# Low parts of streamed weight tiles: a negated copy and an accumulating DMA in place of a subtraction

## The chip, the cores and the metric

The kernel runs on one core of a Trainium2 chip. The metric is the device time in microseconds of one execution; the median of three runs before the change is 2350.99 us (2349.08 to 2353.13).

The engines are named as in the profile: PE (TensorE, the matmuls), PEld (its weight loads), DVE (VectorE), ACT (ScalarE), POOL (GpSimd), SP (SyncE, which only issues DMAs). Each engine works through its own instructions in program order. A DMA is issued by an engine and then moved by the core's 16 DMA engines.

## What is computed

One inference step of a two-layer backbone on 640 tokens (128 context, 512 latent) of width 2048. Each layer is

```python
h = x * (1 + scale) + shift              # modulation by the conditioning vectors
z = h @ w_in_l                           # 2048 x 6656, split into 12 parts
att    = windowed attention(aq, ak, av, sink, cached context)
hg_out = bidirectional gated scan(hq, hi, hff, hfb)
cv_out = silu(layer_norm(depthwise_conv31(ca * sigmoid(cb))))
mix = concat([att * silu(ag), hg_out * silu(hgate), cv_out * silu(cgate)])
out = mix @ w_out_l                      # 2048 x 2048
x_new = layer_norm(ALPHA * x + gate * out, ln_w_l, ln_b_l)
```

and the modulation vectors come from `silu(cond) @ ada_w + ada_b`. All data are float32.

## The kernel before, in words

**Matmuls in three products.** PE multiplies in the type `float32r`. To keep the precision of float32, each operand is held as a high part (the value cast to `float32r`) and a low part (the value less the high part), and three products are added in PSUM: high by high, high by low, low by high. The activations are kept so in `HH` and `HL`; the weights are streamed, and each streamed tile is split when it has arrived.

**The weight stream.** `w_in` comes as 52 column tiles per layer, 128 output columns each, and each of these as four quarters of 128 x 512 (256 KB). `w_load1` takes one of eight raw slots (`raw`) and has SP load a quarter into it; `w_split` takes two of sixteen slots (`wh`), lets ACT write the high part (line 285) and DVE or POOL subtract it from the raw quarter to get the low part (line 286), and gives the raw slot back. `mm` then does the matmuls of a quarter: four blocks of 128 rows, three products, each on 256 and on 384 tokens (lines 1161 and 1163). `o_load` and `o_split` do the same for the 64 tiles of `w_out` per layer.

**The order.** Python generators (the attention, the scan, the convolution, the modulation of later steps) stand in a list, and `pump` advances them a few steps between matmul quarters, so that each engine's instruction order is fixed when the program is built. In the loop over column tiles `i`, after the matmuls of quarter `c`, `ahead(i, c)` splits quarter `c` of tile `i + 1` and loads up to three quarters beyond it. So a quarter is split about three quarters of a tile's matmuls before PE needs it. Before, `ahead` gave the subtraction to POOL for odd quarters and for all quarters while 32 <= i < 46, and to DVE otherwise; `o_split` always used DVE.

**The stages of a layer**, in the order in which PE meets them: the tiles of the scan (four rounds of `hg_main`, whose products are on lines 534 to 567), of the attention (`att`, lines 856 to 942), of the convolution (`e_ca` with 31 taps on DVE, line 1021, then `conv_ln` with its sums over partitions on lines 420 and 421), the gates, and the output projection (line 1413), in groups of 512 output columns. At the start of the output projection POOL loads the residual `Y` with five DMAs of 1 MB (line 1273; `y0y` in layer 0, `y1y` in layer 1). They can start only when the memory of the mixing stage is free. In layer 1, `rows` also has POOL multiply `Y` by the LayerNorm weight and add its bias, group by group (line 1292). Beside all this, DVE computes the modulation of the next steps as row products (`ada_dve`, line 356), whose tiles come through the same raw slots.

In the output projection `feed` splits tile n as soon as the slots of tile n - 8 are free; tiles 0 to 3 are split while PE is still at the last column tile, and tiles 4 to 6 before the first product.

Of the kernel before, what the change touches and what calls it, by code (L numbers as in the profile page):

```python
# [9 lines left out]
F32 = mybir.dt.float32  # L10
# [3 lines left out]
AF = mybir.ActivationFunctionType  # L14
ALU = mybir.AluOpType
# [5 lines left out]
T = 640  # L21
# [68 lines left out]
class Slots(Free):  # L90
    """SBUF slots whose tile is made anew when its type changes."""

# [32 lines left out]
def trunk(ctx: ExitStack, tc: tile.TileContext, A: dict):  # L125
    nc = tc.nc
    act, dve, pool, pe, sync = nc.scalar, nc.vector, nc.gpsimd, nc.tensor, nc.sync
# [74 lines left out]

# [1 line left out]
    sync.dma_start(out=sm, in_=A["small"])  # L204
# [32 lines left out]

# [1 line left out]
    active = []  # L239
# [41 lines left out]
    def split(hi, lo, src, lo_eng=None, hi_eng=None):  # L281
        if hi_eng:
            hi_eng.tensor_copy(hi, src)
        else:
            act.copy(hi, src)  # L285
        (lo_eng or dve).tensor_tensor(lo, src, hi.bitcast(F32), op=ALU.subtract)  # L286

# [1 line left out]
    def adab(l, part):  # L289
        o = SM["adab"] + 48 * l + 16 * part  # L290
        return sm[:, o:o + 16]
# [88 lines left out]

# [1 line left out]
    xq = deque()  # L382
# [16 lines left out]

# [1 line left out]
    act.activation(nsink, sm[:, SM["sink"]:SM["sink"] + 16], AF.Copy, scale=-1.0)  # L401
# [9 lines left out]

# [1 line left out]
    CH = (slice(0, 384), slice(384, T))  # L413
# [10 lines left out]

# [1 line left out]
    HGS = Free([0, 1])  # L426
# [292 lines left out]

# [1 line left out]
    kvres = {}  # L721
# [268 lines left out]

# [1 line left out]
    convs = {}  # L992
# [114 lines left out]

# [1 line left out]
    wraw = {}  # L1109
# [13 lines left out]
    def w_split(l, i, c, lo_eng=None, hi_eng=None):  # L1123
        pump_until(lambda: len(WH.f) >= 2)
        hi, lo = WH.take(), WH.take()
        r = wraw.pop((l, i, c))
        split(hi, lo, r, lo_eng, hi_eng)
        wsp[l, i, c] = (hi, lo)
        RAW.put(r)
# [11 lines left out]
    def o_split(l, t):  # L1141
        pump_until(lambda: len(WH.f) >= 2)
        hi, lo = WH.take(), WH.take()
        r = oraw.pop((l, t))
        split(hi, lo, r)
        osp[l, OT[t][0], OT[t][1]] = (hi, lo)
        RAW.put(r)

# [1 line left out]
    def mm(l, i, z, ks, halves):  # L1150
# [13 lines left out]

# [1 line left out]
    NS = 3  # L1166
# [39 lines left out]
    for l in range(DEPTH):  # L1206
# [16 lines left out]
        first = NS if l == 0 else 2  # L1223
        wnext = 4 * (first + 2)

        def ahead(i, c):
            nonlocal wnext
            m = 4 * (i + 1) + c
            if i + 1 < NN:
                w_split(l, i + 1, c, pool if c % 2 or 32 <= i < 46 else None)  # L1230
            else:
                o_split(l, c)
            while wnext <= m + (WLH if 0 in hold else WLA):
                if wnext < 4 * NN:
                    w_load1(l, wnext // 4, wnext % 4)
                else:
                    o_load(l, wnext - 4 * NN)
                wnext += 1
# [17 lines left out]

# [1 line left out]
        for k in range(KT):  # L1258
# [143 lines left out]
        for gi, (n0c, w) in enumerate(GROUPS[:-1]):  # L1402
# [3 lines left out]
            for k0 in range(0, KT, 2):  # L1406
                for tts, k in [(p, k) for p in ((range(3), range(3, TT)) if k0 == 0 else (range(TT),))
                               for k in (k0, k0 + 1)]:
                    hi, lo = osp[l, gi, k // kper]
                    o = w * (k % kper)  # L1410
                    for tt in tts:
                        for n_, (h_, w_) in enumerate(((HH, hi), (HH, lo), (HL, hi))):
                            pe.matmul(bs[tt][:, 0:w], lhsT=h_[:, tt, k, :], rhs=w_[:, o:o + w],  # L1413
                                      start=(k == 0 and n_ == 0), stop=(k == KT - 1 and n_ == 2))
# [28 lines left out]
        for tt in range(TT):  # L1443
            b = banks.popleft() if last else obank[tt]
            for k in range(KT):
                hi, lo = osp[l, gi, k // 2]
                o = w * (k % 2)
                for n_, (h_, w_) in enumerate(((HH, hi), (HH, lo), (HL, hi))):
                    pe.matmul(b[:, 0:w], lhsT=h_[:, tt, k, :], rhs=w_[:, o:o + w],
                              start=(k == 0 and n_ == 0), stop=(k == KT - 1 and n_ == 2))  # L1450
# [133 lines left out]
```

## Time and profile before

| | |
|---|---|
| median of the runs | 2350.99 us |
| span of the profiled execution | 2354.9 us |
| PE busy | 2211.0 us (94%) |
| PE weight loads busy | 2101.6 us (89%) |
| DVE busy | 1788.6 us (76%) |
| ACT busy | 894.0 us (38%) |
| POOL busy | 718.6 us (31%) |
| mean granted TensorE clock | 0.976 |

The profiled execution spans 2354.9 us, 3.9 us above the median of the runs. The shares are means over stages with different limits; which engine is waited for is read stage by stage. Issuing a DMA does not count as busy.

### The profile page before, as it was taken

To read this page: it belongs to the slowest core of one execution; us is meant where nothing else is said; L and a number is where in the kernel's file an instruction comes from. 1 tells how busy PE (TensorE), PEld (TensorE's weight loads), DVE (VectorE), ACT (ScalarE), POOL (GpSimd) and SP (SyncE) were. 2 spreads that over 40 slices of the span, in tenths; PEclk is the share of its full clock that TensorE was granted. 3 is DMA by queue.
4 is the path that set the end of the run, shared out by engine and by line. 5 is a ranking of instruction groups with operands and counts; after the bars stand their busy time and mean duration, and the time that the engine had idled before them with its cause. 6 is when DMAs were issued, how large, how long until landed. Compare 5 with 4: busy or idle time off the path is not lost.

```text
span 2354.9 us, 41512 instructions
## 1 busy us (share of the span) xinstructions
PE 2211.0 (94%) x15854; PEld 2101.6 (89%) x15854; DVE 1788.6 (76%) x3890; ACT 894.0 (38%) x1647; POOL 718.6 (31%) x540
## 2 busy tenths in 40 slices
PE   6898989999999986999998999999999999999996
PEld 3598989998999986978898999999999999998886
DVE  3488899778869999976576788886776799856547
ACT  1165655423443221431125466653344421251111
POOL 0034244321223444300003343343222255524125
PEclk9999999999999998999999999999999999999998
DMA  9933343443432233564433233333333132335333
GB/s 368 396 118 124 113 126 114 138 138 108 127 95 81 95 103 102 154 235 149 131 117 126 90 106 107 94 103 116 108 104 93 53 97 63 95 92 190 103 88 114
DMA packets 151351, 298.67 MB, mean 127 GB/s; under 512 B 17936, under 2 KB 23792, under 8 KB 149232
## 3 DMA queue, kind: packets, MB, share of 16 engines
q1 hardware_dynamic: 138992, 271.85, 36.0%
q10 hardware_dynamic: 9920, 12.10, 1.7%
q0 software_dynamic: 2240, 12.08, 1.3%
q8 instruction: 124, 2.03, 0.4%
q14 instruction: 75, 0.61, 0.1%
HBM read 278.61 MB, written 12.11 MB: 123 GB/s over the span
## 4 chain that ended last, share of the span: by engine, by line
PE 40%; DVE 25%; issue 3%; ACT 2%; DMA 0%; POOL 0%; ACTq 0%; SPq 0%; DVEq 0%; POOLq 0%
PE z L1163 12%; DVE s L1021 11%; PE z L1413 8%; PE z L1161 8%; PE m L1413 7%; DVE junk L356 5%; DVE wh L286 1%; PE m L856 1%; PE m L942 1%; DVE s L528 1%; DVE y1y L1382 1%; DVE s L527 1%; ACT s L1360 1%; DVE y1y L1383 0%; ACT wh L285 0%
## 5 line engine op out<-in xcount | busy, mean ns | idle before, releaser
L1163 PE MATMUL z<-HH,wh 128*128 128x384 f32 x3296 | 1055.9, 341 | 0.0
L1161 PE MATMUL z<-HH,wh 128*128 128x256 f32 x3296 | 934.7, 285 | 10.8 <-DVE s L1010 6.5
L286 POOL TENSOR_TENSOR wh<-raw,wh 128x512 fp32r<-128x512 f32 x256 | 387.1, 1519 | 893.2 <-ACT wh L285 637.8
L1161 PEld LDWEIGHTS z<-HH,wh 128*128 128x128 f32 x3296 | 627.9, 191 | 15.5 <-issue 5.0
L356 DVE SCALAR_TENSOR_TENSOR junk<-raw,s 128x256 bf16<-128x256 f32 x1024 | 617.1, 603 | 26.1 <-DMA raw<-adawD 4.0
L1163 PEld LDWEIGHTS z<-HH,wh 128*128 128x128 f32 x3296 | 627.2, 190 | 1.5
L1163 PE MATMUL z<-HL,wh 128*128 128x384 f32 x1648 | 561.9, 341 | 0.0
L285 ACT CAST wh<-raw 128x512 fp32r<-128x512 f32 x536 | 319.6, 617 | 520.1 <-PE m L1413 135.7
L286 DVE TENSOR_TENSOR wh<-raw,wh 128x512 fp32r<-128x512 f32 x288 | 260.7, 916 | 287.2 <-ACT wh L285 283.3
L1161 PE MATMUL z<-HL,wh 128*128 128x256 f32 x1648 | 465.2, 282 | 0.0
L1161 PEld LDWEIGHTS z<-HL,wh 128*128 128x128 f32 x1648 | 315.3, 191 | 0.0
L1163 PEld LDWEIGHTS z<-HL,wh 128*128 128x128 f32 x1648 | 313.5, 190 | 0.0
L1021 DVE SCALAR_TENSOR_TENSOR s<-s,sm,s 128x655 f32<-128x655 f32 x240 | 288.4, 1202 | 6.3
L1413 PE MATMUL z<-wh,HH 128*128 128x512 f32 (+1 forms) x768 | 207.8, 357 | 7.3 <-ACT s L1090 5.5
L1413 PEld LDWEIGHTS z<-wh,HH 128*128 128x128 f32 x768 | 137.3, 191 | 28.4 <-ACT s L1090 5.8
L1413 PE MATMUL m<-wh,HH 128*128 128x512 f32 (+1 forms) x512 | 150.9, 376 | 0.0
L1413 PE MATMUL z<-wh,HL 128*128 128x512 f32 (+1 forms) x384 | 136.8, 356 | 0.0
L1413 PEld LDWEIGHTS m<-wh,HH 128*128 128x128 f32 x512 | 94.2, 188 | 17.7
L1413 PE MATMUL m<-wh,HL 128*128 128x512 f32 (+1 forms) x256 | 96.2, 376 | 0.0
L1292 POOL TENSOR_TENSOR y1y<-y1y,s 128x2560 f32<-128x2560 f32 (+1 forms) x10 | 48.4, 4838 | 120.7 <-DMA s<-lnw_r 104.5
L356 DVE DVE_READ_ACCUMULATOR junk<-raw,s 128x1 f32 x1024 | 82.8, 81 | 0.0
L1413 PEld LDWEIGHTS z<-wh,HL 128*128 128x128 f32 x384 | 73.3, 191 | 10.3
(553 smaller groups left out, 2577.9 us busy)
## 6 DMA issues: line engine op xcount, KB each, us to landing
raw<-win SPq DMA_DIRECT2D x416, 256.0 KB, 2.7
raw<-adawD SPq DMA_DIRECT2D x256, 256.0 KB, 2.7
x<-adaw SPq DMA_DIRECT2D x64, 512.0 KB, 8.3
raw<-wout SPq DMA_DIRECT2D x128, 256.0 KB, 2.8
s<-crow SPq DMA_DIRECT2D x32, 256.0 KB, 4.0
s<-xT ACTq DMA_DIRECT2D x16, 320.0 KB, 7.3
s<-s ACTq DMA_DIRECT2D x80, 64.0 KB, 2.1
y0y<-xr POOLq DMA_DIRECT2D x5, 1024.0 KB, 10.9
```

Of the source, the lines that this page charges most:

```text
L285: act.copy(hi, src)
L286: (lo_eng or dve).tensor_tensor(lo, src, hi.bitcast(F32), op=ALU.subtract)
L356: dve.scalar_tensor_tensor(junk, r[:, 256 * n:256 * n + 256], 1.0, rows[0][:, 256 * c:256 * c + 256], op0=ALU.mult, op1=ALU.mult, accum_ou ...
L527: dve.tensor_tensor(o, o, cap(Kt, 0, [[T + h, 2], [2 * h, nb], [1, h]]), op=ALU.mult)
L528: dve.scalar_tensor_tensor(er[:, 0:T], er[:, 0:T], SC, q, op0=ALU.mult, op1=ALU.mult)
L856: pe.matmul(b[:, 0:w], lhsT=a_, rhs=k_, start=(n_ == 0), stop=(n_ == 2))
L942: pe.matmul(o, lhsT=v_, rhs=p_, start=(y == 0 and n_ == 0), stop=(y == len(bl) - 1 and n_ == 2))
L1021: dve.scalar_tensor_tensor(acc, u[:, t:t + AW], sm[:, cw + t:cw + t + 1], acc, op0=ALU.mult, op1=ALU.add)
L1161: pe.matmul(za, lhsT=w_, rhs=h_[:, 0:2, k, :], start=st_, stop=sp_)
L1163: pe.matmul(zb, lhsT=w_, rhs=h_[:, 2:5, k, :], start=st_, stop=sp_)
L1292: pool.tensor_tensor(yv, yv, s[:, 0:w].unsqueeze(1).to_broadcast([P, TT, w]), op=op)
L1413: pe.matmul(bs[tt][:, 0:w], lhsT=h_[:, tt, k, :], rhs=w_[:, o:o + w], start=(k == 0 and n_ == 0), stop=(k == KT - 1 and n_ == 2))
```

## The change

`split_add` is new. ACT writes the high part as before, then writes the negated high part into the low slot, and POOL issues a DMA that adds the raw tile to what stands there. It is used for every quarter that `ahead` splits and for every tile of `w_out`: 516 tiles. The 28 quarters that are split elsewhere (16 at the start of layer 0, 12 between the layers) keep the subtraction.

```diff
+    def split_add(hi, lo, r):
+        act.copy(hi, r)
+        act.activation(lo, hi.bitcast(F32), AF.Copy, scale=-1.0)
+        pool.dma_start(out=lo.bitcast(F32), in_=r, accum_op=ALU.add)
...
-        split(hi, lo, r, lo_eng, hi_eng)
+        if lo_eng == "dma":
+            split_add(hi, lo, r)
+        else:
+            split(hi, lo, r, lo_eng, hi_eng)
         wsp[l, i, c] = (hi, lo)
...
         r = oraw.pop((l, t))
-        split(hi, lo, r)
+        split_add(hi, lo, r)
         osp[l, OT[t][0], OT[t][1]] = (hi, lo)
...
             if i + 1 < NN:
-                w_split(l, i + 1, c, pool if c % 2 or 32 <= i < 46 else None)
+                w_split(l, i + 1, c, "dma")
             else:
                 o_split(l, c)
```

What this does to the order is seen on two engines. On POOL, at the start of layer 1's output projection, before the change (`a10v` and `a10k` are tiles of the mixing stage, `y1y` is the residual):

```order
L1097 TENSOR_TENSOR a10v<-a10v,s_12476 128x640
L286 TENSOR_TENSOR wh_17546<-raw_246,wh_621 128x512
L286 TENSOR_TENSOR wh_239<-raw_250,wh_238 128x512
L1273 DMA y1y<-n_107 128x2048 x5
L1292 TENSOR_TENSOR y1y<-y1y,s_19266 128x5x512
L1292 TENSOR_TENSOR y1y<-y1y,s_19268 128x5x512
```

and at the same place after it (line 291 is the accumulating DMA, lines 1281 and 1300 are the former 1273 and 1292):

```order
L291 DMA wh_413<-raw_164 128x512
L291 DMA wh_234<-raw_516 128x512
L291 DMA wh_417<-raw_166 128x512
L1281 DMA y1y<-n_107 128x2048 x5
L291 DMA wh_618<-raw_248 128x512
L291 DMA wh_17947<-raw_246 128x512
L291 DMA wh_17980<-raw_518 128x512
L1300 TENSOR_TENSOR y1y<-y1y,s_19725 128x5x512
L1300 TENSOR_TENSOR y1y<-y1y,s_19727 128x5x512
L291 DMA wh_239<-raw_250 128x512
L291 DMA wh_7542<-raw_162 128x512
```

POOL had nothing of the weights behind the five loads of the residual; now the low parts of tiles 4, 5 and 6 (the three rows under `y1y<-n`) are issued behind them, and those of tile 7 and later behind the two passes over the residual as well. In layer 0 the loads of `y0y` stand ahead of the same tiles, without the passes.

On ACT, in a round of the scan in layer 0, before the change:

```order
L285 CAST wh_416<-raw_164 128x512
L651 COPY s_117<-m_103 128x512
L651 COPY s_133<-m_104 128x512
L285 CAST wh_617<-raw_166 128x512
L661 COPY s_141<-m_101 128x128
```

and at the same place after it (line 289 is the cast, line 290 the negated copy; the copies out of PSUM on lines 656 and 666 are the former 651 and 661):

```order
L289 CAST wh_416<-raw_164 128x512
L290 ACTIVATE wh_417<-wh_416 128x512
L656 COPY s_117<-m_103 128x512
L656 COPY s_133<-m_104 128x512
L289 CAST wh_617<-raw_166 128x512
L290 ACTIVATE wh_618<-wh_617 128x512
L666 COPY s_141<-m_101 128x128
```

Behind each cast ACT has a second instruction of the same size, which waits for the first, and the copies of the scan, which stood behind the cast, now stand behind both.

## Rows read from the trace of the kernel before

**Rows 1.** The page, section 1: the span.

```profile
span 2354.9 us, 41512 instructions
```

**Rows 2.** Windows: length; busy (x) of PE, PEld, DVE, ACT, POOL; PEclk, DMA, GB/s.

```profile
150.00:420.00 270.00, 241.65 (x2240) 236.40 (x2239) 247.31 (x597) 152.74 (x246) 96.58 (x77) 0.95 0.39 119
420.00:740.00 320.00, 311.68 (x2111) 307.89 (x2110) 246.67 (x731) 124.11 (x286) 81.42 (x65) 0.98 0.38 115
740.00:965.00 225.00, 194.07 (x1278) 190.99 (x1277) 218.81 (x413) 50.36 (x87) 93.63 (x75) 0.94 0.32 102
965.00:1025.00 60.00, 54.48 (x352) 53.25 (x351) 56.90 (x179) 27.19 (x43) 12.95 (x8) 0.96 0.55 171
...
1310.00:1580.00 270.00, 263.99 (x2486) 260.49 (x2486) 225.67 (x416) 166.63 (x270) 112.23 (x89) 1.00 0.34 102
```

**Rows 3.** Windows, one of 50 us in layer 1's convolution stage, same columns.

```profile
1950.00:2000.00 50.00, 50.00 (x343) 50.00 (x342) 48.62 (x39) 11.09 (x20) 32.50 (x20) 1.00 0.21 64
```

**Rows 4.** Waits of PE: instruction, whom it waited for, us in total, times, longest.

```profile
PE m L534 <- DVE s L601: 19.5, 10, 3.4
PE m L420 <- ACT s L285: 13.5, 1, 13.5
...
PE m L856 <- DVE ats L871: 8.7, 4, 4.0
...
PE z L1161 <- POOL wh L286: 1.5, 3, 0.5
```

**Rows 5.** Groups by line: form, count, busy us, mean ns, idle before and its releasers.

```profile
L286 POOL TENSOR_TENSOR wh<-raw,wh 128x512 fp32r<-128x512 f32 x256 | 387.1, 1519 | 893.2 <-ACT wh L285 637.8 <-PE z L1163 156.0 <-issue 66.6
L285 ACT CAST wh<-raw 128x512 fp32r<-128x512 f32 x536 | 319.6, 617 | 520.1 <-PE m L1413 135.7 <-PE z L1413 132.1 <-DMA raw<-win 125.9
...
L286 DVE TENSOR_TENSOR wh<-raw,wh 128x512 fp32r<-128x512 f32 x288 | 260.7, 916 | 287.2 <-ACT wh L285 283.3 <-DMA s<-gsc 2.7 <-issue 0.5
...
L874 ACT ACTIVATE wh<-wh,ats 128x512 f32<-128x512 f32 (+2 forms) x50 | 30.4, 609 | 110.0 <-DVE ats L871 110.0
```

**Rows 6.** Timeline of DVE around 1926 to 1952 us: start, length, instructions merged.

```profile
1925.72 17.60 DVE L1021 SCALAR_TENSOR_TENSOR s<-s,sm,s 128x655 f32<-128x655 f32 x11
...
1946.44 5.58 DVE L1021 SCALAR_TENSOR_TENSOR s<-s,sm,s 128x655 f32<-128x655 f32 x6
```

**Rows 7.** Timeline of POOL in the same stretch, up to its last instruction there.

```profile
1927.71 7.50 POOL L286 TENSOR_TENSOR wh<-raw,wh 128x512 fp32r<-128x512 f32 x4 [8.41 <-ACT wh L285]
...
1935.30 5.48 POOL L286 TENSOR_TENSOR wh<-raw,wh 128x512 fp32r<-128x512 f32 x3
1940.94 1.68 POOL L286 TENSOR_TENSOR wh<-raw,wh 128x512 fp32r<-128x512 f32 x1 [0.17 <-ACT wh L285]
```

**Rows 8.** Line 286 on POOL from 740 to 920 us: durations in ns (min/median/max).

```profile
L286 POOL TENSOR_TENSOR wh<-raw,wh x42: 1275/1406/2004, 743.0 to 915.8; 128x512 fp32r<-128x512 f32 x42
```

**Rows 9.** The same line on POOL from 150 to 420 us.

```profile
L286 POOL TENSOR_TENSOR wh<-raw,wh x27: 1277/1469/1983, 161.3 to 411.1; 128x512 fp32r<-128x512 f32 x27
```

**Rows 10.** DMA issues: queue, count, KB each, median us from issue to landing.

```profile
raw<-win SPq DMA_DIRECT2D x416, 256.0 KB, 2.7
...
s<-s ACTq DMA_DIRECT2D x80, 64.0 KB, 2.1
```

**Rows 11.** Line 1273 (POOL's loads of the residual): durations in ns, then landing.

```profile
L1273 POOL DMA_DIRECT2D y0y<-xr x5: 540/540/594, 1032.2 to 1034.4; - x5
...
DMA to landing us min/median/max: 5.7/10.9/16.9
```

**Rows 12.** Timeline of POOL in layer 1's output projection.

```profile
2116.89 2.73 POOL L1273 DMA_DIRECT2D y1y<-n  x5 [26.98 <-issue]
2135.41 11.86 POOL L1292 TENSOR_TENSOR y1y<-y1y,s 128x2560 f32<-128x2560 f32 x2 [15.78 <-DMA y1y<-n]
```

**Rows 13.** The chain, stretches 1010 to 1060 and 2105 to 2140: start, length, work.

```profile
1037.20 2.72 PE z L1413 x12
...
2125.93 2.72 PE z L1413 x12
```

## Prediction

> **What bounds the kernel now.** I read the windows by stage first, then PE's waits, then the other engines in the stretches where PE waits. The profiled execution spans 2354.9 us [rows 1], 3.9 us above the median of the runs (2350.99); the sum below is made against the span and then moved down by those 3.9 us. In most of layer 1 PE is the limit: in a convolution stretch it is busy for 50.00 of 50 us although DVE is at 48.62 [rows 3]. What can be won stands in layer 0 [rows 2]: PE is idle for 28.4 of 270 us in the scan (150 to 420), 8.3 of 320 in the attention, 30.9 of 225 around the convolution, 5.5 of 60 before the output projection, and 6.0 of 270 in layer 1's scan: 79 us. PE's waits say for whom [rows 4]: in the scan DVE (line 601 above all), in the attention DVE (line 871), and after the convolution the cast of line 285, which waits for the last taps. DVE is busy for 247 of 270, 247 of 320 and 219 of 225 us in the three stretches. The granted clock is 0.95, 0.98 and 0.94 there, and 1.00 in layer 1's scan: between its two levels, 1.2 and 2.4 GHz, some 67 us pass at the lower one, next to the idle times.
>
> **What DVE gets back.** Of its 288 subtractions 266 go, at 916 ns [rows 5]: 244 us. POOL loses 250 of 256, at 1519 ns. That second removal matters for DVE too. In layer 1's convolution six taps in a row take 5.58 us, 0.93 each, when POOL is still; eleven taken just before, while POOL makes eight subtractions, take 17.60 us, 1.60 each [rows 6, 7]. 17.60 less 11 x 0.93 is 7.4 us, so a subtraction on POOL makes DVE about 0.9 us slower. From 740 to 920 us POOL makes 42 of them [rows 8]: 39 us of slowing, so DVE's 219 us at the convolution become 180 of 225 (80%). From 150 to 420 it makes 27 [rows 9], worth 25 us, and as even quarters go to DVE, as many of DVE's own go, another 25: 197 of 270 (73%). In layer 1's scan DVE is busy for 226 of 270 us (84%) and PE idle for only 6 [rows 2], so PE should there become the limit. I take 26 of 28.4 us in layer 0's scan, 25 of 30.9 at the convolution (some latency remains behind the last tap), 5 of 8.3 in the attention, 3 of 5.5 before the projection, 2 of 6.0 in layer 1's scan, where ACT gets fuller. With 7 us for time at the lower clock that goes with the gaps (33 at most: half of 67), the gain is 68 us; its bounds are 0 and 79 + 33.
>
> **What is added.** ACT gets 516 negated copies. The nearest rows are its cast, 617 ns, and an activation of the same size, 609 ns [rows 5]: 315 us, from 894 to about 1,210, 51% of the span. POOL gets 516 issues at 540 ns [rows 11], less than the subtractions took. The accumulating DMA itself no row shows. Below: a 256 KB load lands after 2.7 us, and 64 KB from SBUF to SBUF after 2.1 [rows 10]. Above: 1 MB lands after 5.7 us when nothing is ahead of it [rows 11]. It has to read source and target, so I take 4 us, the middle, and keep 2.7 and 8.
>
> The Trainium skill (Collectives: The Full Stack, "The bandwidth ceiling: the fold count and why AG ≠ RS ≠ AR") says that a reducing DMA is slower only because it reads two sources, not for the addition. No run here shows it. By that page the moving part would double: 64 KB more cost (2.7 - 2.1) / 3 = 0.2 us, so 256 KB would land at about 3.5 us, an estimate, and the sum would be about 1 us better.
>
> **What hides it.** A column tile is 96 matmuls; at 343 in 50 us [rows 3] that is 14.0 us. A quarter is split three quarters of a tile ahead, 10.5 us. Cast, copy, issue and landing make 0.6 + 0.6 + 0.5 + 4 = 5.7 us, so 4.8 us are left for waits in queues. Before, half of the quarters already stood in POOL's queue behind the scan's and the attention's work, and PE waited 1.5 us in all for POOL's low parts [rows 4]. I put 4 us on new waits of this kind, and 1 us on the four copies ahead of the projection's casts on ACT.
>
> **Where it isn't hidden.** At the start of the output projection POOL issues the five residual loads and, behind them, the low parts of tiles 4 to 6. The loads are issued within 2.7 us but land after 5.7, 10.9 (median) and 16.9 us [rows 11, 12]: one after the other, about 2.8 us each. A DMA that POOL issues behind them will land behind them. In layer 0 the last load is issued at 1034.4, so the data are there at about 1051, tile 4's low part at about 1053; PE starts tile 4 at 1037.20 and needs it 0.2 us later [rows 13]. That is a wait of 15 us; since the loads wait for DVE's last gate, which will be less late, I take 13. In layer 1 the passes over the residual start when its loads have landed, at 2135.41 [rows 12], so tile 4's low part is there at about 2137, and PE starts it at 2125.93 [rows 13]: 11 us. The passes then hold POOL until 2147.3, so tile 7's low part lands at 2147.3 + 0.5 + 4 = 2151.8; at 3.4 us per tile (15 matmuls at 2.72 / 12 us) PE would want it at 2136.3. Together 15 us. What is late next: nothing, since the slots of the tiles behind have come free meanwhile. The later passes, 12 us for each group, are queued when PE is at the group's ninth tile, and the low part behind them is wanted eight tiles, 27 us, later: covered. Long waits lower the clock: in the stretch with the 13.5 us for line 285 it is 0.94, 27 of 225 us at the lower level [rows 2, 4], more than the wait itself; I take 5 us for both. The last tiles, split only when the eighth tile before them is done and then used in quick succession, cost 1 us per layer. Loss: 13 + 15 + 5 + 2 + 4 + 1 = 40 us.
>
> **Sum.** 68 - 40 = 28 us: a span of 2327, a median of 2323 us. Its own range, with half of the unsure shares of the gain (20 us) and the landing between 2.7 and 8 us: 2303 to 2345.
>
> **The rivals.**
> - *The waits at the projections are not there* (accumulating DMAs get past the loads, or the mixing stage ends so much earlier that the loads are through). Against: the five landings in turn, and in layer 1 DVE was not late, so nothing ends earlier. Then of the losses 7 us remain: 2351 - 68 + 7 = 2290. The Trainium skill (DMA: Bandwidth & Descriptors, "SWDGE vs HWDGE vs iDMA") says that only one queue is allocated to the DMAs that GpSimd issues; by that rule the first half of this rival cannot happen, and the landings agree.
> - *Gains and losses meet*: the scan of layer 0 keeps most of its idle time because its steps wait for each other, not for DVE's load. 2323 + 26 = 2349.
> - *ACT becomes the limit of the scan* (slower). A round of the scan has 16 splits, so ACT gets 9.8 us more per round, in line with its exponentials and copies out of PSUM; in layer 1 it goes from 167 of 270 us to about 205 [rows 2]. If half of it lies on the chain, 5 us in each of eight rounds, layer 0 gains 20 us less and layer 1 loses 22 more: 2365. From 3.5 us per round on, the change loses. For it: casts wait for raw tiles, and a raw slot now comes free some 3 us later, so ACT waits in order too. Against: ACT is still idle for a quarter of the stage.
> - *The accumulating DMA is slow* (slower): if its packets take so long that a tile needs more than PE's 3.4 us in the output projection, PE waits at some 120 tiles; at 5.4 us per tile this is 240 us, 2560. If only its landing is late, 8 us instead of 4, the two waits grow by 4 each and some quarters at the end of layer 0's convolution, which are split late, cost about 10: 2341; it decides from about 12 us.
>
> **Chances.** The forecast 0.55, no waits at the projections 0.10, gains and losses meet 0.08, ACT as the limit 0.15, a slow DMA 0.12. A measurement of this kernel tells about 0.2% (4.7 us) from no change: faster 0.65, same 0.08, slower 0.27. The range reaches down to the first rival and up past ACT's half case: 2285 to 2390.
>
> **What the profile will show.** Right: layer 0's scan and convolution with PE idle for under 10 us each, DVE near 80%, and the taps at 0.93 us almost throughout; two waits of PE of 10 to 16 us for an accumulating DMA, one soon after each start of the output projection, and a second piece in layer 1 behind line 1300. ACT near 1,210 us. Wrong: PE waiting for ACT in the scan's rounds; accumulating DMAs that land after more than 8 us away from the residual loads; or no wait at the residual loads, in which case the time is below 2303.

## The result and the profile after

The changed kernel takes 2296.7 us in the median (four runs, 2296.3 to 2298.2), the kernel before 2350.95 on the same chip: ratio 0.9765, 95% interval 0.9753 to 0.9777, 54 us less. The forecast was 2323, with 2303 to 2345 as its own range: the direction is right, and the gain is about twice the 28 us foreseen. The time lies below that range, and inside the 2285 to 2390 that the forecast kept open for its rivals.

The page of the changed kernel, its span and the engines' busy time (share of the span, instructions):

```profile
span 2295.2 us, 42650 instructions
...
PE 2187.4 (95%) x15854; PEld 2081.0 (91%) x15854; DVE 1369.6 (60%) x3624; ACT 1217.7 (53%) x2163; POOL 753.5 (33%) x806
```

The profiled spans differ by 59.7 us (2354.9 [rows 1] to 2295.2). DVE is busy for 1,370 us instead of 1,789. ACT is at 1,217.7, where 1,210 was expected. On POOL the issues of the accumulating DMAs do count as busy in this view: they are 453.9 of its 753.5 us (below).

Windows of the changed kernel, with the columns of [rows 2]. Both kernels give PE the same instructions in the same order, so each window begins at the PE instruction that begins the stage before:

```profile
148.56:385.73 237.17, 229.05 (x2238) 225.47 (x2238) 208.94 (x553) 185.40 (x297) 94.90 (x103) 1.00 0.76 189
385.73:695.41 309.68, 306.64 (x2110) 303.90 (x2110) 203.47 (x716) 174.05 (x368) 84.85 (x96) 0.99 0.76 184
695.41:881.34 185.93, 185.93 (x1278) 185.88 (x1277) 175.79 (x403) 79.25 (x134) 63.54 (x80) 1.00 0.80 193
881.34:943.36 62.02, 54.12 (x350) 52.96 (x350) 50.03 (x172) 36.29 (x58) 16.05 (x17) 0.94 0.89 237
943.36:1080.84 137.48, 127.39 (x550) 104.64 (x548) 51.84 (x184) 50.60 (x83) 37.27 (x45) 0.96 0.92 234
...
1244.48:1509.46 264.98, 263.34 (x2486) 260.38 (x2485) 152.47 (x368) 207.59 (x333) 110.35 (x121) 1.00 0.70 163
...
2036.51:2079.96 43.45, 32.47 (x138) 26.10 (x138) 6.93 (x10) 17.50 (x30) 23.73 (x18) 0.88 0.73 211
```

Read against [rows 2] (length less PE's busy time is its idle time; the bounds of those rows moved by up to 0.25 us to the same PE instructions): layer 0's scan takes 237.2 us instead of 269.9 with 8.1 idle, the attention 309.7 instead of 320.0 with 3.0 idle, the convolution 185.9 instead of 225.1 with no idle time at all, layer 1's scan 265.0 instead of 269.9. PE's clock is 1.00, 0.99 and 1.00 in layer 0's three stages, where it was 0.95, 0.98 and 0.94. The fourth row is the first that loses: 62.0 us up to the start of layer 0's output projection, before 60.1.

For the projections' first stretches, which had no row yet, the kernel before, same columns:

```profile
1025.25:1150.14 124.89, 124.89 (x549) 103.31 (x548) 78.90 (x230) 25.75 (x42) 2.73 (x5) 0.99 0.53 179
...
2110.07:2140.05 29.98, 29.98 (x139) 25.14 (x139) 15.20 (x19) 10.50 (x18) 7.37 (x6) 1.00 0.68 264
```

The first 125 us of layer 0's projection became 137.5, the rest up to layer 1's tiles 163.6 (160.0), and the stretch in which layer 1's projection starts 43.5 (30.0); in between, 3.0 us were won in 530. With 1.6 us won ahead of the first row and 0.4 lost behind the last, 91.7 us were won and 32.0 lost.

PE's waits in the changed kernel, to be read against [rows 4]:

```profile
PE z L1421 <- DMA wh<-raw: 20.4, 3, 9.7
...
PE z L1421 <- ACT s L1095: 8.1, 2, 7.9
...
PE m L539 <- DVE s L606: 4.6, 5, 1.4
```

The waits for DVE's lines 606 and 876 (601 and 871 before) fell from 19.5 to 4.6 and from 8.7 to 3.0 us, and the one for the sums behind the convolution is gone. New are three for an accumulating DMA (`wh<-raw`), and 8.1 us for ACT's line 1095, the last gate.

The groups by line of POOL's new issues, DVE's row products of the modulation, and its taps (count | busy us, mean ns | idle before), then the latter two of the kernel before:

```profile
L291 POOL DMA_DIRECT2D wh<-raw x516 | 453.9, 959 | 1352.3 <-ACT wh L290 1243.1
...
L361 DVE SCALAR_TENSOR_TENSOR junk<-raw,s 128x256 bf16<-128x256 f32 x1024 | 506.6, 495 | 172.2 <-DMA raw<-adawD 141.8
...
L1026 DVE SCALAR_TENSOR_TENSOR s<-s,sm,s 128x655 f32<-128x655 f32 x240 | 224.3, 935 | 6.3
```

```profile
L356 DVE SCALAR_TENSOR_TENSOR junk<-raw,s 128x256 bf16<-128x256 f32 x1024 | 617.1, 603 | 26.1 <-DMA raw<-adawD 4.0
...
L1021 DVE SCALAR_TENSOR_TENSOR s<-s,sm,s 128x655 f32<-128x655 f32 x240 | 288.4, 1202 | 6.3
```

A tap took 1,202 ns in the mean before, a row product 603. Both are faster now, where the forecast had measured taps alone. POOL's issues take 0.86 us in the median (below), not 0.54, and 453.9 us together, more than the 387.1 of the subtractions [rows 5].

The accumulating DMAs up to layer 0's output projection (durations of the issue in ns, then issue to landing), and the landing of the three that are issued behind the residual loads there:

```profile
L291 POOL DMA_DIRECT2D wh<-raw x195: 849/860/1868, 132.4 to 929.0; - x195
...
DMA to landing us min/median/max: 3.2/4.6/8.5
...
DMA to landing us min/median/max: 14.8/15.5/16.3
```

The timeline of POOL at the start of layer 0's projection and of its passes over the residual in layer 1, and PE's first instruction after the first wait (start, length, in brackets the idle time before):

```profile
947.10 2.65 POOL L1281 DMA_DIRECT2D y0y<-xr  x5 [17.20 <-issue]
949.74 2.71 POOL L291 DMA_DIRECT2D wh<-raw  x3
...
2061.16 11.46 POOL L1300 TENSOR_TENSOR y1y<-y1y,s 128x2560 f32<-128x2560 f32 x2 [11.04 <-DMA y1y<-n]
```

```profile
964.58 0.80 PE L1421 MATMUL z<-wh,HH 128*128 128x512 f32 x1 [9.70 <-DMA wh<-raw]
```

This is the forecast mechanism: five loads, then three accumulating DMAs, the first of which is issued at 949.74 and lands 14.8 us later, when PE goes on. In layer 1 line 1300 then holds POOL for 11.46 us, to 2072.6, and PE waits for a second piece, 1.6 us.

### The profile page after: what moved, and what is told of

Read it like the earlier page. It is cut to its first block, busy times and chain, and to the rows that moved or that the text cites. A ratio compares the mean times of both kernels' runs of the same rounds, so it can differ in the third digit from the quotient of the medians.

```text
span 2295.2 us, 42650 instructions
## 1 busy us (share of the span) xinstructions
PE 2187.4 (95%) x15854; PEld 2081.0 (91%) x15854; DVE 1369.6 (60%) x3624; ACT 1217.7 (53%) x2163; POOL 753.5 (33%) x806
## 4 chain that ended last, share of the span: by engine, by line
PE 70%; DVE 10%; issue 7%; DMA 7%; ACT 3%; POOL 2%; ACTq 0%; SPq 0%; POOLq 0%; DVEq 0%
PE z L1171 32%; PE z L1169 21%; PE z L1421 5%; PE m L1421 4%; DVE junk L361 4%; DMA x<-adaw 2%; PE m L947 2%; PE m L861 2%; POOL wh L291 1%; DMA wh<-raw 1%; DMA s<-xT 1%; PE m L915 1%; DVE HL L286 1%; DMA raw<-win 1%; PE m L663 1%
## 5 line engine op out<-in xcount | busy, mean ns | idle before, releaser
L1171 PE MATMUL z<-HH,wh 128*128 128x384 f32 x3296 | 1045.4, 338 | 0.0
L1169 PE MATMUL z<-HH,wh 128*128 128x256 f32 x3296 | 924.7, 282 | 0.9 <-DVE wh L286 0.9
L291 POOL DMA_DIRECT2D wh<-raw x516 | 453.9, 959 | 1352.3 <-ACT wh L290 1243.1
L1169 PEld LDWEIGHTS z<-HH,wh 128*128 128x128 f32 x3296 | 618.2, 188 | 4.4 <-DVE wh L286 1.6
L1171 PEld LDWEIGHTS z<-HH,wh 128*128 128x128 f32 x3296 | 619.4, 188 | 1.5
L361 DVE SCALAR_TENSOR_TENSOR junk<-raw,s 128x256 bf16<-128x256 f32 x1024 | 506.6, 495 | 172.2 <-DMA raw<-adawD 141.8
L290 ACT ACTIVATE wh<-wh 128x512 fp32r<-128x512 f32 x516 | 326.4, 632 | 73.7 <-PE z L1171 59.0
L1169 PEld LDWEIGHTS z<-HL,wh 128*128 128x128 f32 x1648 | 310.2, 188 | 0.0
L1171 PEld LDWEIGHTS z<-HL,wh 128*128 128x128 f32 x1648 | 309.9, 188 | 0.0
L1026 DVE SCALAR_TENSOR_TENSOR s<-s,sm,s 128x655 f32<-128x655 f32 x240 | 224.3, 935 | 6.3
L1421 PEld LDWEIGHTS m<-wh,HH 128*128 128x128 f32 x512 | 94.7, 189 | 18.1 <-DMA wh<-raw 0.3
L1095 ACT ACTIVATE s<-z 128x640 f32<-128x640 f32 x32 | 22.5, 702 | 132.1 <-PE z L1171 121.2
```

Of the source, the lines that this page charges most:

```text
L290: act.activation(lo, hi.bitcast(F32), AF.Copy, scale=-1.0)
L291: pool.dma_start(out=lo.bitcast(F32), in_=r, accum_op=ALU.add)
L361: dve.scalar_tensor_tensor(junk, r[:, 256 * n:256 * n + 256], 1.0, rows[0][:, 256 * c:256 * c + 256], op0=ALU.mult, op1=ALU.mult, accum_ou ...
L1026: dve.scalar_tensor_tensor(acc, u[:, t:t + AW], sm[:, cw + t:cw + t + 1], acc, op0=ALU.mult, op1=ALU.add)
L1169: pe.matmul(za, lhsT=w_, rhs=h_[:, 0:2, k, :], start=st_, stop=sp_)
L1171: pe.matmul(zb, lhsT=w_, rhs=h_[:, 2:5, k, :], start=st_, stop=sp_)
```

## The experiments

In the diffs, `wl` is the third argument of `w_split` in `ahead`, which is `"dma"` in the changed kernel; `o_split` on `split` means DVE's subtraction in the output projection as before. Each time is a median, with the ratio to runs of the kernel before on the same chip (2351.3 to 2353.2).

**1. Whose subtractions mattered.** Two kernels, each with one half of the change, and one with no accumulating DMA at all.

```diff
 e1_dve_half    wl: pool if c % 2 or 32 <= i < 46 else "dma"      o_split: split
 e2_pool_half   wl: "dma" if c % 2 or 32 <= i < 46 else None      o_split: split
 e9_all_on_dve  wl: None (DVE subtracts)                          o_split: split
```

> Of the streamed weight quarters only those whose low part DVE subtracted before get the negated copy and the accumulating DMA; those that POOL subtracted stay on POOL, and the output projection's quarters stay on DVE. In the convolution tiles (32 to 45) every quarter was POOL's, so nothing changes there. Theory 1 (POOL's subtractions slow DVE, and that holds PE back): of the 84 us that the change gains up to the output projection of layer 0, about half of the scan's 33 and of the attention's 11 come, and under 10 of the convolution's 39; nothing is lost at the projections; together a gain of about 25 to 35 us, 2316 to 2326. Theory 2 (DVE's own subtractions were the load, POOL's cost DVE nothing, and the convolution was late only because DVE came into it late): nearly all 84 us come, about 2265.

> The other half: only the streamed quarters that POOL subtracted before get the negated copy and the accumulating DMA; those that DVE subtracted stay on DVE, and the output projection's quarters too. DVE has not one subtraction fewer than before. Theory 1 (POOL's subtractions slow DVE): the taps fall from a mean of 1.2 us to about 0.93, the convolution gains about 35 of its 39 us and the scan and the attention about half of theirs; about 2351 - 58 = 2293. Theory 2 (only DVE's own subtractions count): DVE's busy time and the time stay within 10 us of before, 2341 or more.

> No accumulating DMA at all: DVE makes every low part of the streamed quarters and of the output projection's, also the 240 odd that POOL made before. Theory 1 (a subtraction on POOL costs DVE about as much time as one of DVE's own, 0.7 to 0.9 us against 0.92): DVE's busy time stays near the 1,790 us of before, the taps fall to about 0.93 us, and the time stays within 25 us of before, 2330 to 2375. Theory 2 (the order of POOL's and DVE's work, not DVE's load, held PE back; DVE's own subtractions were worth nothing when e1_dve_half took them away): at least half of the gain of e2_pool_half comes, 2310 or less.

Measured: *e1_dve_half* 2354.8 us (1.0012, interval 1.0002 to 1.0022), *e2_pool_half* 2267.8 (0.9639, 0.9624 to 0.9653), *e9_all_on_dve* 2311.8 (0.9830, 0.9812 to 0.9847). Of *e1_dve_half* the taps, and the window of layer 0's scan (columns of [rows 2]):

```profile
L1026 DVE SCALAR_TENSOR_TENSOR s<-s,sm,s 128x655 f32<-128x655 f32 x240 | 290.9, 1212 | 6.3
```

```profile
150.33:424.58 274.25, 241.24 (x2239) 236.89 (x2239) 240.49 (x554) 169.18 (x272) 113.06 (x102) 0.93 0.54 140
```

Of *e2_pool_half* DVE's subtractions and taps, and the scan and the convolution:

```profile
L286 DVE TENSOR_TENSOR wh<-raw,wh 128x512 fp32r<-128x512 f32 x288 | 256.4, 901 | 349.4 <-ACT wh L285 347.4
...
L1026 DVE SCALAR_TENSOR_TENSOR s<-s,sm,s 128x655 f32<-128x655 f32 x240 | 223.5, 931 | 6.3
```

```profile
150.18:393.88 243.70, 232.13 (x2239) 228.00 (x2238) 218.74 (x591) 168.59 (x270) 73.81 (x74) 0.99 0.59 158
...
703.41:889.34 185.93, 185.93 (x1278) 185.88 (x1277) 176.83 (x407) 76.08 (x129) 60.42 (x75) 1.00 0.79 189
```

To take 138 subtractions from DVE alone gave nothing: the taps stay at 1.21 us, the scan is 4 us longer than before (why, no run settles), the attention 8 us shorter, the convolution 2 us longer (227.0). DVE's busy time fell by only 51 us (1,788.6 to 1,738.0) although the subtractions that went had taken 118: beside POOL's, the row products took 657 ns in the mean instead of 603. To take the 250 from POOL, with all 288 of DVE's left where they were, gave more than the whole change (the waits at the projections, number 3, are missing here): the scan takes 243.7 us, the convolution 185.9 with no idle time, as in the changed kernel. Theory 1's direction holds against theory 2, but its halves are wrong: POOL's half alone gives nearly all of it. DVE's busy time fell by 206 us (1,788.6 to 1,582.6) without one instruction less, 0.82 us for each subtraction that POOL no longer makes.

Of *e9_all_on_dve* DVE's subtractions, their durations (min/median/max, ns) before the change, and the convolution's window:

```profile
L286 DVE TENSOR_TENSOR wh<-raw,wh 128x512 fp32r<-128x512 f32 x538 | 422.8, 793 | 389.4 <-ACT wh L285 366.6
```

```profile
L286 DVE TENSOR_TENSOR wh<-raw,wh x288: 673/691/6214, 30.1 to 2305.7; 128x512 fp32r<-128x512 f32 x144
```

```profile
720.30:924.96 204.66, 193.58 (x1278) 190.15 (x1277) 199.77 (x462) 52.06 (x88) 23.35 (x25) 0.98 0.37 113
```

Even with 250 subtractions more, DVE is busy for less time than before (1,695.5 us). A subtraction of its own takes 0.69 us in the median, before the change too; the mean of 0.92 [rows 5] is raised by a few, up to 6.2 us long, that run beside line 1292's passes in layer 1's projection. The 250 added take 166.4 us more than in *e2_pool_half*, 0.67 each. The time lies between the two expectations, 18 us below theory 1's range and 2 above theory 2's: a subtraction on POOL (0.82 us of DVE's time) was dearer for DVE than one of its own, not "about as dear". At the convolution DVE is at 199.8 of 204.7 us and PE is idle for 11, so there DVE's load does decide.

**2. POOL's work put back without its use.** On *e3_projection_plain* (number 3), POOL gets one extra instruction per quarter in the convolution tiles.

```diff
                 w_split(l, i + 1, c, "dma")
+                if 32 <= i < 46:
+                    pool.tensor_tensor(cos, cos, <ones>, op=ALU.mult)           # e4_pool_ballast
+                    pool.tensor_scalar(cos, cos, 1.0, None, op0=ALU.mult)       # e11_pool_reads_one
+                    pool.memset(lo, 0.0)  (ahead of ACT's negated copy)         # e10_pool_writes_only
```

> The kernel of e3_projection_plain, and in the convolution tiles (32 to 45 of each layer) POOL also makes, for each quarter, an elementwise product of two 128x512 operands that nothing waits for (a table times ones, in place). The low parts still come by DMA. Theory 1 (POOL's elementwise work slows DVE, and that was what held PE back at the convolution): the taps go back to about 1.2 us in the mean, PE waits again around layer 0's convolution, and 25 to 39 us of the gain are lost: 2297 to 2311, beside 2272 without it. Theory 2 (the time before went to low parts that POOL finished late): within 5 us of e3_projection_plain.

> As e4_pool_ballast (2361), but POOL's instruction reads one operand of 128x512 instead of two (a table times the constant 1, in place). Theory 1 (what POOL reads slows DVE, and it holds DVE up for as long as the instruction runs): its duration falls well under the 1.72 us of the product, the taps' mean lies between 0.94 and 1.36 in proportion to POOL's time, and some 92 us x (its duration / 1.72) are lost, less whatever DVE can take without PE waiting: 2275 to 2330. Theory 2 (only two operands on both sides collide): taps at 0.94 us, 2268.

> The kernel of e3_projection_plain, and in the convolution tiles POOL fills each low part with zeros before ACT writes the negated high part: 112 instructions of 128x512 on POOL that read nothing. ACT's copy waits for the fill, which is an extra of under 1 us in a path that has several to spare. Theory 1 (only what POOL reads from SBUF slows DVE's instructions with two operands): taps near 0.94 us in the mean, time within 8 us of e3_projection_plain (2268). Theory 2 (any elementwise work of POOL slows DVE for as long as it runs): taps above 1.1 us, 2290 or more.

Measured: *e4_pool_ballast* 2360.8 us (1.0043, 1.0027 to 1.0059), *e11_pool_reads_one* 2298.2 (0.9771, 0.9750 to 0.9792), *e10_pool_writes_only* 2266.9 (0.9638, 0.9617 to 0.9658), beside 2268.3 without an extra instruction. The taps of the three in this order, for the first with the window of layer 0's convolution and two of PE's waits, for the second with the extra instruction:

```profile
L1026 DVE SCALAR_TENSOR_TENSOR s<-s,sm,s 128x655 f32<-128x655 f32 x240 | 327.4, 1364 | 6.3
```

```profile
697.95:948.79 250.84, 203.94 (x1278) 200.69 (x1277) 244.46 (x414) 82.13 (x138) 118.55 (x123) 0.89 0.61 145
```

```profile
PE m L379 <- DVE s L372: 21.1, 1, 21.1
...
PE z L1169 <- DMA wh<-raw: 9.2, 4, 2.9
```

```profile
L1026 DVE SCALAR_TENSOR_TENSOR s<-s,sm,s 128x655 f32<-128x655 f32 x240 | 262.9, 1096 | 6.3
...
L1240 POOL TENSOR_SCALAR cos<-cos 128x512 f32<-128x512 f32 x112 | 220.8, 1972 | 0.1
```

```profile
L1028 DVE SCALAR_TENSOR_TENSOR s<-s,sm,s 128x655 f32<-128x655 f32 x240 | 224.3, 935 | 6.3
```

The product takes back the whole gain: PE is idle for 46.9 of 250.8 us at layer 0's convolution, at a clock of 0.89, and for 24.8 us between layer 1's scan and its projection, which the expectation did not foresee (92 us lost instead of 25 to 39). Most of the latter is one wait of 21.1 us for DVE's part of the modulation (line 372); that it comes late because of the slower taps is likely, but not shown. Not all of the loss goes by way of DVE: for 9.2 us PE waits for low parts whose DMAs POOL issues behind the products. That is not the main path, since *e11_pool_reads_one* holds POOL longer and loses a third of it. DVE's busy time grows by 144 us (1,485.0 to 1,629.1), 1.29 us for each of the 112 products; by 0.56 us (62.9 in all) for each instruction that reads one operand, although those are longer on POOL (1.97 us); by nothing for a fill (0.73 us each). So it is what POOL reads that slows DVE.

A tap and the extra instruction that it met, first of *e4_pool_ballast*, then of *e11_pool_reads_one* (two taps; the second met it):

```profile
789.23 2.58 DVE L1026 SCALAR_TENSOR_TENSOR s<-s,sm,s 128x655 f32<-128x655 f32 x1
...
789.50 1.60 POOL L1241 TENSOR_TENSOR cos<-cos,ones 128x512 f32<-128x512 f32 x1
```

```profile
731.85 2.58 DVE L1026 SCALAR_TENSOR_TENSOR s<-s,sm,s 128x655 f32<-128x655 f32 x2
...
732.80 1.82 POOL L1240 TENSOR_SCALAR cos<-cos 128x512 f32<-128x512 f32 x1
```

The Trainium skill (SBUF — State Buffer, "SBUF: two separate sides") says that VectorE and GpSimd share a pair of ports, and that a VectorE instruction with two SBUF inputs collides with a GpSimd instruction that reads SBUF, not with one that only writes. The fill that costs nothing agrees. The Trainium skill there also calls it an exclusive lock, so that the loser is blocked for the whole instruction. The means above can't tell, as they count all 112 instructions, whether they met one of DVE's or not. The single tap of *e4_pool_ballast* agrees: it lasts 2.58 us, where the median is 0.90, so 1.68 more beside a product of 1.60, and the ten other taps that a whole product fell into last 1.6 to 1.9 us more. The two of *e11_pool_reads_one* don't: 2.58 us instead of 1.80 is 0.78 more beside an instruction of 1.82. For one operand the measurement decides: DVE loses part of the instruction, not all.

**3. The waits at the projections.**

```diff
 e3_projection_plain   o_split:  split_add(hi, lo, r)  ->  split(hi, lo, r)
 e5_residual_on_sync   line 1281:  pool.dma_start(out=Y[:, tt, :], ...)  ->  sync.dma_start(...)
 e12_low_parts_first   the loop of line 1281 moved behind the first feed(), so behind the low parts of tiles 4 to 6
```

> All streamed quarters by the accumulating DMA, the output projection's quarters by DVE's subtraction as before. Theory 1 (PE's waits of 9.7, 9.2 and 1.6 us at the start of the two output projections come from accumulating DMAs that stand behind the residual loads in POOL's DMA queue, and the clock costs some 4 us with them): the waits go, and the time is 2297 - 25 = 2272. Theory 2 (PE waits there for something that is late anyway, such as raw tiles or slots, because all 16 DMA engines are busier): half or less of the waits goes, 2285 or more.

> The changed kernel with only the five residual loads of each layer moved from POOL to SP, so that they no longer stand ahead of accumulating DMAs in POOL's queue; the same 5 MB move at the same time. Theory 1 (the queue: a DMA of POOL lands behind those issued before it): the low part of the fourth tile lands some 4 to 5 us after its issue, PE's waits of 9.7 and 9.2 us for it go or fall under 2 us; the raw tiles that now stand behind the residual loads on SP are late instead, from the seventh tile on, for up to 10 us per layer: 2275 to 2297. Theory 2 (the traffic: 16 DMA engines busy with the residual delay everything): the accumulating DMAs land as late as before (7.6 us in the median there, up to 16), PE waits as long for them, 2290 to 2305.

> The changed kernel with one thing moved: POOL issues the low parts of the output projection's tiles 4 to 6 ahead of the five residual loads, not behind them. The same bytes move at the same time. In e5_residual_on_sync these low parts landed 10.2 to 15.5 us after their issue although the loads had gone to another queue, in the changed kernel 14.8 to 16.3. Theory 1 (the order in the queue and on the DMA engines decides: who is issued first is moved first): they land after 4 to 7 us, PE's waits of 9.7 and 9.2 us at the fourth tile fall under 2 us each, and what is issued behind the loads (tile 7 and later) makes PE wait for at most half of what was saved: 2275 to 2288. Theory 2 (the 5 MB of residual in flight share all 16 DMA engines evenly, whoever was issued first): they still land after 9 us or more, and the time stays within 6 us of the changed kernel, 2291 to 2303.

Measured: *e3_projection_plain* 2268.3 us (0.9645, 0.9631 to 0.9660), as theory 1 said: 28 us below the changed kernel. *e5_residual_on_sync* 2308.3 (0.9814, 0.9798 to 0.9831) and *e12_low_parts_first* 2306.4 (0.9810, 0.9794 to 0.9826) are both slower than the changed kernel. In *e5_residual_on_sync*, in layer 0, the issues of the five loads on SP, the landing of the three low parts of tiles 4 to 6 (issued at 948.88, 950.05 and 951.22), and that of the third alone:

```profile
L1281 SPq DMA_DIRECT2D y0y<-xr x5: 328/434/798, 948.3 to 950.5; - x5
...
DMA to landing us min/median/max: 10.2/12.8/15.5
...
DMA to landing us min/median/max: 15.5/15.5/15.5
```

The landing of the same three tiles' low parts in *e12_low_parts_first*, in layer 1, and PE's waits for low parts in that kernel:

```profile
DMA to landing us min/median/max: 3.3/3.8/5.5
```

```profile
PE z L1421 <- DMA wh<-raw: 24.4, 2, 18.1
```

Issued ahead of the loads, the first low part lands after 3.3 us (3.5 in layer 0), and the wait at the fourth tile is gone; behind them in the same queue it lands after 14.8. With the loads in SP's queue the first, issued behind two of them, takes 10.2, and the third, issued behind all five, 15.5, as long as the three in the changed kernel (14.8 to 16.3). So what counts is how much was issued ahead, in whichever queue; these runs show no part that the queue alone would have. The waits only became shorter in layer 0 (6.5 us in three pieces and 6.4 in one, where there were 9.7), and in layer 1 they are longer: 17.1 and 18.1 us in one piece, for low parts that POOL issues after line 1300's passes, which begin later (at 2067.6 us in *e12_low_parts_first* instead of 2061.2). The first part of theory 1 holds in *e12_low_parts_first*, the saving that it foresaw does not.

**4. The price of the accumulation and of the copy.** Both on *e3_projection_plain*.

```diff
 e6_plain_copy       -        pool.dma_start(out=lo, in_=r, accum_op=ALU.add)
                     +        pool.dma_start(out=lo, in_=r)
 e7_no_copy_on_act   as e6_plain_copy, and
                     -        act.activation(lo, hi, AF.Copy, scale=-1.0)
```

> The kernel of e3_projection_plain with the accumulation taken off the DMA: it copies the raw tile over the negated high part (so the low parts hold the whole weight). Same bytes written, one source less to read. Theory 1 (an accumulating DMA costs its second source): the landing falls from 4.3 us in the median to 3 to 3.5, and the share of the 16 DMA engines for POOL's queue by about half. Theory 2 (the landing is the queue and the issue): it stays within 0.3 us. In both the time stays within 5 us of e3_projection_plain (2268), since the landing is hidden; if accumulation had a price in the scan's rounds, it would fall by more.

> The kernel of e6_plain_copy without the negated copy on ACT (the DMA writes the low part alone). ACT's busy time falls by about 245 us, to about 895. Theory 1 (the copies are hidden): the time stays within 5 us of e6_plain_copy. Theory 2 (the copies cost: in the scan's rounds, and at PE's wait of 7.6 us for ACT's last gate ahead of layer 0's output projection): 8 to 15 us faster than e6_plain_copy, about 2255.

Measured: *e6_plain_copy* 2254.9 us (0.9586, 0.9572 to 0.9601), *e7_no_copy_on_act* 2248.4 (0.9559, 0.9545 to 0.9573). POOL's queue (packets, MB, share of 16 engines) and landing, first of *e3_projection_plain*, then of *e6_plain_copy*:

```profile
q0 software_dynamic: 58112, 113.81, 28.3%
...
wh<-raw POOLq DMA_DIRECT2D x388, 256.0 KB, 4.3
```

```profile
q0 software_dynamic: 33280, 113.81, 13.2%
...
wh<-raw POOLq DMA_DIRECT2D x388, 256.0 KB, 2.9
```

The landing falls from 4.3 to 2.9 us and the queue's share to under half, as theory 1 said. The rule of the Trainium skill that the prediction named (Collectives: The Full Stack, "The bandwidth ceiling: the fold count and why AG ≠ RS ≠ AR": two sources to read, not the addition) agrees with this, though the runs can't tell reading from adding; the estimate of 3.5 us that the prediction worked out from it was too low. But "hidden" was wrong for both: accumulating costs 13 us, the copies on ACT (245 us of its time) another 6.5, above 5 but below theory 2's 8. Of the 13, 8.8 lie in the stretch before layer 0's projection (61.9 us in *e3_projection_plain*, 53.2 here), and number 5 shows how; of the 6.5, 4.6 lie in layer 0's scan.

**5. Where the rest was lost, and a better version.**

```diff
 e8_plain_at_the_end   wl: "dma" if c % 2 or i < 46 else None      o_split: split
```

> Where e2_pool_half and e3_projection_plain each lost something: the accumulating DMA for all streamed quarters up to tile 45, behind that only for those that POOL subtracted before, DVE's subtraction for the others and for the output projection. Theory 1 (the raw slots that the accumulating DMA holds some 5 us longer make the output projection's first raw tiles late, ACT casts HH only behind them, and the last gate behind that): HH's casts of layer 0 start earlier, the 7.6 us of PE's wait for the last gate fall to about 2, and the scan keeps what e3 gained over e2: 2261 to 2264. Theory 2 (the lead over e2 is given back there because HH's casts hang on other things): as e2 and e3, 2266 to 2269.

Measured: 2259.4 us (0.9607, 0.9592 to 0.9621), 37 us below the changed kernel; only *e6_plain_copy* and *e7_no_copy_on_act*, which leave part of the low parts' work out, are faster. ACT's timeline before layer 0's projection, first of *e3_projection_plain*, then of *e8_plain_at_the_end* (its first cast of `HH`, and the last gate), and the window of the latter that answers to the fourth row above:

```profile
928.73 0.61 ACT L285 CAST HH<-a00op 128x512 fp32r<-128x512 f32 x1
...
938.32 0.70 ACT L1095 ACTIVATE s<-z 128x640 f32<-128x640 f32 x1
```

```profile
921.25 0.61 ACT L285 CAST HH<-a00op 128x512 fp32r<-128x512 f32 x1
...
931.60 0.71 ACT L1095 ACTIVATE s<-z 128x640 f32<-128x640 f32 x1
```

```profile
881.83:934.99 53.16, 52.36 (x350) 51.65 (x350) 49.80 (x174) 30.68 (x49) 8.55 (x8) 1.00 0.76 218
```

ACT casts `HH` behind the casts of the projection's first raw tiles and makes the last gate behind them. A raw slot that an accumulating DMA still reads comes free later (in the changed kernel SP's loads of raw tiles wait 1,068.9 us for such DMAs, 300 times), the tiles come later, and so does all that stands behind them. With fewer accumulating DMAs at the end the casts of `HH` begin at 921.25 instead of 928.73, the gate at 931.60 instead of 938.32, and the stretch takes 53.2 us with 0.8 idle, against 62.0 in the changed kernel. SP issues the load of the projection's third raw tile at 923.20 us in *e3_projection_plain* and at 914.01 in *e8_plain_at_the_end*. That it is the accumulating and not ACT's copies, of which there are 20 fewer here, *e6_plain_copy* shows: it has all the copies and no accumulating, and its stretch takes 53.2 us too. Theory 1 is right, the time a little below its range.

## Why the prediction came out as it did

The mechanism was right and several sizes were not; one half of it was nearly empty. That the time fell in the lower end of the wide range, kept open for a rival that did not come, is luck.

- **What DVE gets back.** The 250 subtractions that POOL loses are nearly all of it: *e2_pool_half*. Of DVE's own, 118 more are gone in *e8_plain_at_the_end* than there, for 8.4 us (2267.8 to 2259.4), 6.5 of them in the scan (243.7 to 237.2); while POOL goes on they are worth nothing (*e1_dve_half*). In the changed kernel's scan DVE is at 208.9 us, not at the 197 foreseen; one of its own there is 0.69 us, not the mean of 0.92. The 0.9 us per subtraction, from eleven taps, was good: 0.82 in *e2_pool_half*. In the changed kernel the same rate needs 175 us, 419 less 244, over 250: 0.70.
- **PE's idle time.** Foreseen 26, 25, 5, 3 and 2 us; by the windows 20.2, 30.9, 5.3, -2.4 and 4.4. "Some latency remains behind the last tap" was too careful: DVE at 175.8 of 185.9 us (the forecast said 180) leaves PE no idle time at all.
- **The clock: the term that was mis-sized.** It stood at 7 us, "33 at most". In layer 0's three stages 82.2 us were won and only 56.4 of them were idle time; by the other 25.8 PE's busy time fell for the same matmuls (747.4 us to 721.6), and the granted clock is 0.99 to 1.00 now. With the gaps the low clock goes almost altogether. This is most of the 24 us by which the gain came out larger (91.7 less 68); the other 8 us of the 32 between forecast and measured span are losses that were put too high (32.0 against 40). That the clock makes the whole of the 25.8 is not shown: at the convolution of *e9_all_on_dve* PE's busy time is 7.7 us above 185.9 at a clock of 0.98, which can make at most some 4 us of 204.7.
- **The landing.** 4 us taken, 4.5 measured, bounds 2.7 and 8. The split was 5.7 us by the forecast and has 10.5: PE waits for a low part of the streamed tiles only at the projections, so the 4 us for new waits in queues were not needed. The cost lay in the raw slots, which the forecast named under ACT only: 7.9 us at the last gate.
- **The projections.** Layer 0: 15, taken as 13, against one wait of 9.7. Layer 1: 15 in two pieces against 9.2 and 1.6. The clock beside them 5, and 5.0 by the windows (12.6 + 13.5 longer, 21.1 of it idle). Issuing for 0.86 us instead of 0.54 shows in no wait of PE's. "Behind them in the queue" is not the reason that the runs show: with the loads in another queue the low part behind all five lands just as late (*e5_residual_on_sync*).
- **Losses not foreseen**: the last gate, which *e3_projection_plain* still has (7.6 us) and *e8_plain_at_the_end* has not (0.8), and 3.7 us behind layer 0's projection, 3.4 of them idle, which with the projection's subtraction on DVE are gone (*e3_projection_plain*). By PE's waits the latter are 1.8 us more for DVE's line 1309, 1.0 for ACT's line 1352 and 0.6 for the last low parts; why the first two come late, no run tells.
- **The rivals.** No waits at the projections: the waits are there, yet the time fell below 2303, which the forecast had named as the sign of this rival; it was mostly the clock instead. ACT as the limit: PE waits for ACT in no round of the scan; its copies cost 6.5 us in all. A slow DMA: 13 us for its second source, not decisive.

## What to carry to other kernels

A subtraction handed to POOL "because it is idle" can cost DVE more than doing it (0.82 us against 0.67 here), and at a stage where DVE is the limit it costs that in full; look at the same DVE instruction with POOL busy and still. When idle time of PE goes, count the matmuls at the lower clock with it: here up to a third of what layer 0's three stages won. An accumulating DMA takes work from both engines, but it holds its source's slot until it has landed and waits behind whatever bulk loads were issued ahead of it; where loads of several MB start, keep the subtraction on DVE.

## What the runs showed of the hardware

- POOL slows DVE by what it reads: 1.29 us in the mean for each product of two 128x512 operands, 0.56 for one operand although it takes longer, nothing for a fill. A tap of 0.90 us that met a whole product of 1.60 took 2.58.
- An accumulating DMA of 256 KB between SBUF tiles lands 4.3 us after its issue and takes 64 packets more than a plain copy of the same bytes (58,112 against 33,280 for 388 of them), which lands after 2.9.
- A DMA of 256 KB that is issued behind five loads of 1 MB lands 14.8 to 16.3 us after its issue in the same queue and 15.5 with the loads in another, behind two of them after 10.2, ahead of them after 3.3 to 3.5.
